# Six temporary tiles, a changed first entry, and q chunks that alternate with gate chunks

## The chip, the cores and the metric

The kernel runs on one core of one Trainium2 chip: one TensorE (PE), one VectorE (DVE), one ScalarE (ACT), one GpSimd (POOL), and SyncE (SP), which issues all the DMAs here. The metric is the device time of one launch in microseconds (us). One profiled execution of the kernel before gives the spans, waits and durations that are quoted.

## The reference

The model has four layers on 1040 tokens (16 meta tokens and 1024 tokens of x) of width 1024. Layers 0 and 3 are sliding-window attention, layer 1 is an mLSTM, layer 2 is an HGRN2 (a gated linear recurrence). Each layer normalizes, runs its mixer, and adds to the residual:

```python
for i in range(DEPTH):
    u = rmsnorm(h, norm_gain[i])
    if kind == 0: y = attention_branch(u, ...)
    elif kind == 1: y = mlstm_branch(u, ...)
    else: y = hgrn2_branch(u, ...)
    h = h + jnp.where(valid[None, :, None], y, 0.0)
```

The change touches the first norm, attention and HGRN2. Attention has 16 query heads of 64 on 4 key heads, a window of 128, a learned sink for each head, and a gate z:

```python
q, k, v, z = _split(u @ w_in, (A_W, A_KVW, A_KVW, A_W))
q = rope(rmsnorm(q.reshape(bsz, lp, A_HEADS, A_HD), q_gain), pos)
k = rope(rmsnorm(k.reshape(bsz, lp, A_KV, A_HD), k_gain), pos)
o = sliding_window_attention(q, k, v, sinks, valid)
return (o * jax.nn.silu(z)) @ w_out
```

In HGRN2 a state S of 128 x 128 for each of 8 heads runs through the tokens; a block's output is `q*exp(A) @ S` plus `att @ v` inside the block, and S then becomes `exp(A_last) * S + (k*exp(A_last - A))^T @ v`.

## The kernel before, in words

**Tiling.** The residual x and the normalized u lie transposed: 8 k-tiles of 128 channels by 1040 tokens. Tokens come in three chunks, `(0,400), (400,384), (784,256)`; attention and the recurrences go by 9 blocks of 16 and 8 x 128 tokens. A product of float32 quality is three fp32r products: each operand is split into a high part and a rest (`split`, L194 to L196: ACT casts, DVE subtracts, L196), and PE adds hi x hi, hi x lo and lo x hi. `proj` (L245 to L269) does so for 128 output channels: for each chunk four steps of six matmuls (L262), and with the last step of a chunk an `evac` that takes the sum out of PSUM.

**What sets the order.** The order on PE is written by hand. A step is `[nominal cost, function, weight load]`; lists of steps are laid into each other by `weave` (two lists at even pace), `spread` and `later` (a step at a nominal time), and `chain` (a step some nominal nanoseconds after the matmuls it follows, also into the next list). A function issues all its work on all engines. PE keeps the hand-written order; the instructions of ACT, DVE, POOL and SP are ordered by the framework's scheduler. SP has one DMA queue that goes in order.

**Pools.** `tmp()` hands out tiles of 404 columns, called `t`, and there are five (`TMPS`). `row()` gives one of 8 rows of 1040 columns, `vtile()` one of 10 small v tiles. An instruction that writes a tile waits until the last reader of its former content is done.

**Norm** (L371 to L425). `sq` squares one k-tile of a chunk (ACT, L377) and adds it up (DVE, L381); `stat` sums over the channels by a matmul with a tile of ones (L389), and `rstd_from` makes the inverse root (ACT, Ln L361 and Exp L362); `unit` scales one k-tile (DVE, L415) and splits it into `uh` and `ul`. In the first layer each chunk is summed in two halves, each with its own stat. The ones and the identity for transposes come in one DMA (`const`).

**Attention** (`layer_a`, from L445). A q or k chunk takes three t tiles, `dst`, `sq` and `rot` (the k chunks of the first half use rows). `evac` (L518 to L527) loads cos and sin into the one tile `cs` (L520), scales into `dst` (ACT, L523), squares into `sq` (ACT, L524), and copies `dst` into `rot` with its halves exchanged by four DMAs (L527). Then follow, at the nominal distances `D_Q` of 2000, 4000 and 6000: `stat`, the norm over 64 channels by a matmul with `masks` (L533); `rope` (DVE, L538 to L541); and the split (for q L492 and L493, for k L473 to L476), which is the last reader of the t tiles. The split of q writes one of four buffers (`qs`) for each chunk; where it would come ahead of the S step of the previous pair that last reads that buffer, the last loop of `layer_a` moves it behind that S step.

Pairs of q tiles go through S steps (scores, L624 and L625; DVE adds the mask and takes the maximum, L630; ACT Exp, L633; POOL divides by the sum, L637), T steps (transposes of the scores, L648) and V steps (L667). There are four segments of these steps, one for each pair of q tiles, and each is woven with a `fill`: the projections that will be needed next. `gate_proj` (L436) projects a chunk of z, makes its silu in one t tile (`sigmoid_from`) and multiplies it onto the attention's output row. `proj_out` (L345, L348) is the output product of two tiles.

```python
fills = [
    [tile_of(vg0, vfin0)] + q_pair(1),
    [zs[0], (out1, [(-Y_AHEAD, z) for z in sp1])] + q_pair(2),
    [tile_of(kg1, kfin1), tile_of(vg1, vfin1), zs[1]] + q_pair(3) + [(out3[:cut], ...)],
    [(out3[cut:], []), zs[2]],
]
```

Here `zs[p]` is the gates of pair p, `out1` and `out3` are output products, `kg1` is the k tile of the second half of the key heads, and `q_pair(p)` gives for each chunk both q tiles of pair p.

**HGRN2** (`layer_c`). For each head and each pair of blocks: level steps on DVE and ACT, then the level products on PE (`levels_mm`, L1127 and L1137), then `tail0` (ACT and DVE take the products out, POOL copies parts into `att`, L1165), `tail1` (transposes of k, L1187) and for each of the two blocks `tail2`, called a V step here: `att` times v (L1202), S times q (L1204), k times v (L1209), and the new S by DVE (L1214). The tails of a pair come `TAIL_LAG` = 600 nominal nanoseconds into the list of the next pair.

**Entry.** The first layer's norm of chunk 0 comes alone; the norms of chunks 1 and 2 lie in the projections of chunks 0 and 1, at the shares in `FIRST`. q tiles 0 and 1 and k are projected chunk by chunk ahead of the first S step (`head`); in the first layer all three chunks of q tile 1 come in the third.

Of the kernel before, what the change touches and what calls it, by code (L numbers as in the profile page):

```python
# [15 lines left out]
P = 128  # L16
# [16 lines left out]

C_IDENT, C_ONES = 0, 128
C_W = 256
B_COLS = 96
LOOKAHEAD = 12000.0
TAIL_LAG = 600.0
PRIO = 40
ROWS, TMPS, RAWS, YS = 8, 5, 2, 3  # L40
XS = 14
# [70 lines left out]
def hybrid_kernel(ctx: ExitStack, tc: tile.TileContext, ins, out, layers=(0, 1, 2, 3)):  # L112
# [13 lines left out]
    def nm(x):  # L126
        ctr[0] += 1
        return f"{x}{ctr[0]}"
# [26 lines left out]

    const = cpool.tile([P, C_W], F32, name="const")
    ident = const[:, C_IDENT : C_IDENT + P]
    ones = const[:, C_ONES : C_ONES + P]
    ngain = cpool.tile([P, 4, KT], F32, name="ngain")
# [15 lines left out]
    load_x(0)  # L175
    sp.dma_start(const, ins["const"])
    sp.dma_start(ngain, ins["ngain"])
# [193 lines left out]
    class Norm:  # L371
        def __init__(self, i):
            self.i, self.acc, self.ps = i, {}, {}

        def sq(self, m, n, c0, cn, size=KT):
            q = tmp()[:, :cn]
            s.activation(q, x[:, m, c0 : c0 + cn], AF.Square)  # L377
            if m % size == 0:
                self.acc[n] = q
            else:  # L380
                v.tensor_tensor(self.acc[n], self.acc[n], q, op=ALU.add)  # L381

# [11 lines left out]

        def stats(self, n, parts):

            c0, cn = CHUNKS[n]
            size = KT // parts

            def squares(part):  # L400
                def fn():
                    for m in range(part * size, (part + 1) * size):
                        self.sq(m, n, c0, cn, size)

                return [0.0, fn, None]

            return [z for k in range(parts) for z in (squares(k), self.stat(n, k, parts))]

# [36 lines left out]
    def layer_a(i, j, first, last, fin):  # L445
# [69 lines left out]
        def qk_proj(src, gcol, work, fsplit, ch):  # L515
            late = {}

            def evac(acc, n, c0, cn):  # L518
                cos_sin = R["mix"].tile([P, 2, 400], F32, tag="cs", name=nm("cs"), bufs=1)
                sp.dma_start(cos_sin[:, :, :cn], ins["rope"][:, :, c0 : c0 + cn].rearrange("a p t -> p a t"))  # L520
                dst, sq, rot = work(n, c0, cn)
                late[n] = dst, sq, rot, cos_sin
                s.activation(dst, acc[:, :cn], AF.Identity, scale=R["cons"][:, gcol : gcol + 1])  # L523
                s.activation(sq, acc[:, :cn], AF.Square)  # L524
                for q in range(4):
                    o = q ^ 1
                    sp.dma_start(rot[32 * q : 32 * q + 32], dst[32 * o : 32 * o + 32])  # L527

            def finish(n, c0, cn):
                def stat():  # L530
                    dst, sq, rot, _ = late[n]
                    st = psa()
                    pe.matmul(st[:, :cn], R["masks"][:, 0:P], sq, start=True, stop=True)  # L533
                    rstd_from(st, sq, cn, 64)
# [195 lines left out]
        cut = len(oc[3][0][1]) + 2  # L730
        zs = [(flat(z_pair(p)), []) for p in range(3)]
# [553 lines left out]
    steps = []  # L1285
    norm = Norm(layers[0])

    steps += norm.stats(0, PARTS[0]) + [norm.unit(0, k) for k in range(KT)]
    tail = None
    for pos, i in enumerate(layers):  # L1290
# [30 lines left out]
        else:  # L1321
            h0, h1 = (sum(z[0] for z in head[k]) for k in range(2))
            seq = flat(head)
            for n, t0, t1, end in ((2, h0 + h1 * FIRST[2], h0 + h1 * FIRST[3], h0 + h1), (1, h0 * FIRST[0], h0 * FIRST[1], h0)):
                st = norm.stats(n, PARTS[n])
                later(seq, *((t0 + (t1 - t0) * k / len(st), z) for k, z in enumerate(st)), *norm.units(n, t1, end))
            head = [seq]
# [8 lines left out]
    steps[k][2] = None  # L1336
    load_x(1)
    k = 0
    for n, (cost, fn, pre) in enumerate(steps):
# [30 lines left out]
def _layout(inp):  # L1370
# [3 lines left out]
    f["ngain"] = np.asarray(inp["norm_gain"]).reshape(4, KT, P).transpose(2, 0, 1)  # L1374
    const = np.zeros((P, C_W), np.float32)
    const[:, C_IDENT : C_IDENT + P] = np.eye(P)
    const[:, C_ONES : C_ONES + P] = 1.0
    am = np.zeros((P, 384), np.float32)
# [6 lines left out]
    f["b_mask"] = np.where(ii <= np.arange(P)[None], 0.0, BIG).astype(np.float32)  # L1385
    f["const"] = const
    half = 32
# [76 lines left out]
```

## Time and profile before

| quantity | value |
|---|---|
| median of 3 runs | 2697.6 us (2693.47 to 2699.81) |
| the profiled execution's own time | 2690.46 us |
| its span | 2688.7 us |
| PE busy (matmuls) | 2590.5 us, 96% of the span |
| PE weight loads (PEld), beside the matmuls | 2492.4 us, 93% |
| DVE busy | 1959.5 us, 73% |
| ACT busy | 1693.4 us, 63% |
| POOL busy | 370.1 us, 14% |
| granted TensorE clock, mean | 0.986 |
| moved by DMA | 145.66 MB |

The profiled execution is 7.1 us below the median, or 0.27%. Rows of single instructions give the start in us, the duration in us, the engine, the line, the operation, `out<-in`, the shapes, and in brackets the engine's idle time just ahead and what ended it. Rows of stretches give the length, then busy us and the number of instructions for PE, PEld, DVE, ACT and POOL, then granted clock, DMA share and GB/s. Rows of waits by line, `PE pa L389 <- DVE t L381: 7.0, 2, 4.0`, give the total wait in us, how many, and the longest. Names such as `t`, `r` (a row), `pa`, `pj`, `po`, `pt` (PSUM tiles), `wr`, `wh`, `wl` (weights raw, high, low) are those of the program.

### The profile page before, as it was taken

How to read it: one execution, taken by the hardware profiler on the slowest of the kernel's cores; microseconds unless marked ns; L12 is line 12 of the kernel's file. 1: busy time of each engine (PE TensorE's matmuls, PEld its weight loads, DVE VectorE, ACT ScalarE, POOL GpSimd, SP SyncE). 2: the span in 40 equal slices, each digit the busy share in tenths (PEclk: the TensorE clock that was granted, in tenths of full speed). 3: DMA queues.
4: the chain of work that ended last, by engine and by line, in shares of the span. 5: the costliest groups of instructions: out<-in, count | busy, mean ns of one | idle time of the engine just before them, and what ended most of it. 6: DMA issues, size and time to landing. Idle time of an engine off the chain costs nothing.

```text
span 2688.7 us, 54502 instructions
## 1 busy us (share of the span) xinstructions
PE 2590.5 (96%) x20276; PEld 2492.4 (93%) x20276; DVE 1959.5 (73%) x5337; ACT 1693.4 (63%) x4339; POOL 370.1 (14%) x760
## 2 busy tenths in 40 slices
PE   6899999999999999999999999999999998998999
PEld 5898989999999999999999998999999898898999
DVE  7787687974646474747475688978878978886886
ACT  7776777565454545454545657877676857766772
POOL 0343243000000000000000000101000000541450
PEclk8999999999999999999999999999999999999999
DMA  4223111011111111111111111101111013212212
GB/s 148 84 59 96 52 58 46 21 65 56 40 56 40 56 40 56 40 56 40 56 40 53 51 34 33 34 33 34 41 33 39 31 45 107 69 53 88 73 36 75
DMA packets 89786, 145.66 MB, mean 54 GB/s; under 512 B 12448, under 2 KB 42272, under 8 KB 89520
## 3 DMA queue, kind: packets, MB, share of 16 engines
q1 hardware_dynamic: 89520, 142.17, 16.9%
q8 instruction: 160, 2.62, 0.4%
q14 instruction: 106, 0.87, 0.1%
HBM read 127.28 MB, written 4.26 MB: 49 GB/s over the span
## 4 chain that ended last, share of the span: by engine, by line
PE 72%; DVE 12%; ACT 8%; issue 3%; POOL 2%; DMA 2%; SPq 0%; ACTq 0%; DVEq 0%; POOLq 0%
PE pj L262 35%; PE pj L345 14%; PE pj L307 9%; ACT Sm L633 1%; PE po L667 1%; PE pt L648 1%; PE po L890 1%; POOL Sm L637 1%; PE pa L904 1%; PE po L892 1%; DVE t L415 1%; DVE ul L196 1%; DVE Sm L630 1%; DVE x L348 1%; PE pj L303 1%
## 5 line engine op out<-in xcount | busy, mean ns | idle before, releaser
L262 PE MATMUL pj<-uh,wh 128*128 128x256 f32 (+2 forms) x2688 | 930.5, 346 | 3.4 <-ACT uh L195 3.4
L262 PE MATMUL pj<-ul,wh 128*128 128x256 f32 (+2 forms) x2688 | 871.7, 324 | 3.2 <-DVE ul L196 3.1
L262 PE MATMUL pj<-uh,wl 128*128 128x256 f32 (+2 forms) x2688 | 869.6, 324 | 0.0
L262 PEld LDWEIGHTS pj<-uh,wh 128*128 128x128 f32 x2688 | 513.4, 191 | 24.3 <-issue 6.4
L262 PEld LDWEIGHTS pj<-ul,wh 128*128 128x128 f32 x2688 | 513.7, 191 | 15.2 <-DVE ul L196 5.3
L262 PEld LDWEIGHTS pj<-uh,wl 128*128 128x128 f32 x2688 | 513.2, 191 | 0.1
L637 POOL TENSOR_SCALAR Sm<-Sm,s 128x256 f32<-128x256 f32 (+2 forms) x272 | 254.5, 947 | 410.7 <-DVE s L635 406.0
L196 DVE TENSOR_TENSOR wl<-wr,wh 128x512 fp32r<-128x512 f32 x336 | 228.7, 690 | 54.1 <-ACT wh L195 51.8
L195 ACT CAST wh<-wr 128x512 fp32r<-128x512 f32 x336 | 201.9, 616 | 97.9 <-PE pj L345 27.1
L348 DVE TENSOR_TENSOR x<-x,pj 128x384 f32<-128x384 f32 (+2 forms) x480 | 234.7, 510 | 38.8 <-PE pj L345 37.1
L345 PE MATMUL pj<-yh,wh 128*128 128x384 f32 (+2 forms) x768 | 252.9, 329 | 0.0
L345 PE MATMUL pj<-yl,wh 128*128 128x384 f32 (+2 forms) x768 | 248.0, 323 | 3.3 <-DVE yl L196 3.3
L345 PE MATMUL pj<-yh,wl 128*128 128x384 f32 (+2 forms) x768 | 246.6, 321 | 0.0
L307 PE MATMUL pj<-wh,uh 128*128 128x256 f32 x768 | 231.0, 301 | 0.0
L307 PE MATMUL pj<-wh,ul 128*128 128x256 f32 x768 | 216.4, 282 | 0.0
L307 PE MATMUL pj<-wl,uh 128*128 128x256 f32 x768 | 216.1, 281 | 0.0
L633 ACT ACTIVATE Sm<-Sm,s 128x257 f32<-128x257 f32 (+2 forms) x272 | 130.6, 482 | 84.6 <-DVE s L630 75.5
L432 DVE SCALAR_TENSOR_TENSOR t<-pj,t 128x384 f32<-128x384 f32 (+2 forms) x192 | 99.0, 515 | 107.0 <-ACT t L431 106.5
L433 ACT ACTIVATE t<-t 128x384 f32<-128x384 f32 (+2 forms) x240 | 117.8, 491 | 80.1 <-DVE t L432 79.0
L345 PEld LDWEIGHTS pj<-yl,wh 128*128 128x128 f32 x768 | 145.1, 189 | 5.7 <-DVE yl L196 5.2
L195 ACT CAST yh<-r 128x384 fp32r<-128x384 f32 (+2 forms) x120 | 57.3, 479 | 143.8 <-PE pj L345 126.2
L345 PEld LDWEIGHTS pj<-yh,wh 128*128 128x128 f32 x768 | 145.3, 189 | 1.7 <-DVE S L1214 0.3
(235 smaller groups left out, 5470.9 us busy)
## 6 DMA issues: line engine op xcount, KB each, us to landing
wr<-in_b_win SPq DMA_DIRECT2D x128, 256.0 KB, 2.9
wr<-in_a_win SPq DMA_DIRECT2D x80, 256.0 KB, 2.9
wr<-in_c_win SPq DMA_DIRECT2D x64, 256.0 KB, 2.8
cs<-in_rope SPq DMA_DIRECT2D x28, 384.0 KB, 3.3
wr<-in_a_wout SPq DMA_DIRECT2D x32, 256.0 KB, 2.7
wr<-in_b_wout SPq DMA_DIRECT2D x32, 256.0 KB, 2.7
cs<-in_rope SPq DMA_DIRECT2D x20, 256.0 KB, 2.7
t<-t SPq DMA_DIRECT2D x104, 48.0 KB, 2.2
```

The source lines that it names most:

```text
L195: s.copy(h, src)
L196: v.tensor_tensor(l, src, h.bitcast(F32), op=ALU.subtract)
L262: pe.matmul(acc[:, :cn], a[:, k, :], b[:, k, c0 : c0 + cn], start=(k == 0 and i == 0), stop=(k == KT - 1 and i == 2))
L303: pe.matmul(acc[:48, :256], um[0][:, k, :], m[:, kk, :], start=(k == 0 and m is wh), stop=(k == KT - 1 and m is wl))
L307: pe.matmul(acc[:cn, :256], a[:, k, c0 : c0 + cn], m[:, kk, :], start=(k == 0 and i == 0), stop=(k == KT - 1 and i == 2))
L345: pe.matmul(acc[:, :cn], a[:, k, mc], b, start=(k == 0 and i == 0), stop=(k == 1 and i == 2))
L348: v.tensor_tensor(x[:, m, c0 : c0 + cn], x[:, m, c0 : c0 + cn], acc[:, :cn], op=ALU.add)
L415: v.scalar_tensor_tensor(u, x[:, k, cs], ngain[:, self.i, k : k + 1], self.acc[n], op0=ALU.mult, op1=ALU.mult)
L432: v.scalar_tensor_tensor(a[:, :cn], z, 0.0, a[:, :cn], op0=ALU.min, op1=ALU.subtract)
L433: s.activation(a[:, :cn], a[:, :cn], AF.Exp)
L633: s.activation(Sm[:nq, u, : nk + 1], Sm[:nq, u, : nk + 1], AF.Exp, scale=-1.0, bias=st[:nq, u : u + 1], accum_out=den[:nq, u : u + 1])
L637: g.tensor_scalar(Sm[:nq, u, :nk], Sm[:nq, u, :nk], den[:nq, u : u + 1], None, op0=ALU.mult)
```

## The change

There are six edits in one:

- `TMPS` goes from 5 to 6.
- In segments 1 and 2 of attention the fills use `qz_pair`: each q chunk of pair 2 (or 3) is followed by one gate chunk of pair 0 (or 1). The output product, which stood ahead of the q chunks, now comes behind them.
- The load of `cs` moves from `evac` to the `stat` step of each q or k chunk (L529 of the new file), that is behind the four copies of that chunk.
- `TAIL_LAG` goes from 600 to 2000.
- In the first layer the norm of chunk 0 is summed in four parts instead of two. Those of chunks 1 and 2 are summed in one part each, seven adds on POOL into a row; `FIRST` now holds for each chunk the shares of its squares, its stat and its first unit. The chunks of q tile 1 join the chunks of k and q tile 0. `ones` is made by a memset, and the identity is loaded behind the second part of x.
- In the later norms the sum of chunk 2 lies in a v tile instead of a t tile.

```diff
-TAIL_LAG = 600.0
+TAIL_LAG = 2000.0
-ROWS, TMPS, RAWS, YS = 8, 5, 2, 3
+ROWS, TMPS, RAWS, YS = 8, 6, 2, 3
-PARTS = 2, 2, 2
-FIRST = 0.3, 0.9, 0.3, 0.7
+PARTS = 4
+FIRST = (0.2, 0.8, 0.85), (0.2, 0.75, 0.8)
...
         def sq(self, m, n, c0, cn, size=KT):
-            q = tmp()[:, :cn]
+            if m % size:
+                q = tmp()[:, :cn]
+            elif self.row is not None and n:
+                q = self.row[:, c0 : c0 + cn]
+            else:
+                q = (vtile() if n == 2 else tmp())[:, :cn]
             s.activation(q, x[:, m, c0 : c0 + cn], AF.Square)
             if m % size == 0:
                 self.acc[n] = q
             else:
-                v.tensor_tensor(self.acc[n], self.acc[n], q, op=ALU.add)
+                (v if self.row is None or n == 0 else g).tensor_tensor(self.acc[n], self.acc[n], q, op=ALU.add)
...
             def evac(acc, n, c0, cn):
-                cos_sin = R["mix"].tile([P, 2, 400], F32, tag="cs", name=nm("cs"), bufs=1)
-                sp.dma_start(cos_sin[:, :, :cn], ins["rope"][:, :, c0 : c0 + cn].rearrange("a p t -> p a t"))
...
                 def stat():
-                    dst, sq, rot, _ = late[n]
+                    dst, sq, rot = late[n]
+                    cos_sin = R["mix"].tile([P, 2, 400], F32, tag="cs", name=nm("cs"), bufs=1)
+                    sp.dma_start(cos_sin[:, :, :cn], ins["rope"][:, :, c0 : c0 + cn].rearrange("a p t -> p a t"))
+                    late[n] = dst, sq, rot, cos_sin
...
+        def qz_pair(p, z):
+            (ga, fa), (gb, fb) = qg[2 * p], qg[2 * p + 1]
+            gates = [grp for t in (2 * z, 2 * z + 1) for grp in zc[t]]
+            res = []
+            for n in range(3):
+                for k, (grp, fin) in enumerate(((ga[n], fa[n]), (gb[n], fb[n]))):
+                    res += [tile_of([grp], [fin]), (gates[2 * n + k], [])]
+            return res
...
-            if n == 2:
+            if first:
+                parts += [tile_of([qb[0][n]], [qb[1][n]])]
+            elif n == 2:
                 parts += [tile_of(*qb)]
...
-            [zs[0], (out1, [(-Y_AHEAD, z) for z in sp1])] + q_pair(2),
-            [tile_of(kg1, kfin1), tile_of(vg1, vfin1), zs[1]] + q_pair(3) + [(out3[:cut], [(-Y_AHEAD, z) for z in sp3])],
-            [(out3[cut:], []), zs[2]],
+            qz_pair(2, 0) + [(out1, [(-Y_AHEAD, z) for z in sp1])],
+            [tile_of(kg1, kfin1), tile_of(vg1, vfin1)] + qz_pair(3, 1) + [(out3[:cut], [(-Y_AHEAD, z) for z in sp3])],
+            [(out3[cut:], []), (flat(z_pair(2)), [])],
...
     load_x(1)
+    sp.dma_start(ident, ins["ident"])
```

Three places show how instructions move. A number behind a name counts the tiles; numbers of the two kernels don't correspond.

The first place is PE in the entry, around the first norm matmul of chunk 1 (`pa_235<-t_218,const`). In the kernel before, 24 projection matmuls of chunk 0 stand ahead of it (`pj_211` and `pj_198` are sums of k and q tile 0):

```order
L262 MATMUL pj_211<-uh,wh_112 128x400
L262 MATMUL pj_211<-ul,wh_112 128x400
L262 MATMUL pj_211<-uh,wl_113 128x400
L389 MATMUL pa_235<-t_218,const 128x384
L262 MATMUL pj_198<-uh,wh_94 128x400
L262 MATMUL pj_198<-ul,wh_94 128x400
```

In the changed kernel 60 stand ahead of it: k, q tile 0, and half of q tile 1 (`pj_301`), and the norms of k and q of chunk 0 (L532, with `masks`) come earlier than it:

```order
L259 MATMUL pj_301<-ul,wh_125 128x400
L259 MATMUL pj_301<-uh,wl_126 128x400
L532 MATMUL pa_316<-r_272,masks_205 128x400
L532 MATMUL pa_322<-t_293,masks_205 128x400
L391 MATMUL pa_326<-r_95,ones 128x384
L259 MATMUL pj_301<-uh,wh_125 128x400
```

So the first sum of chunk 1, which now comes from a row (`r_95`) that POOL adds up, is asked for 36 matmuls later, and there is one such matmul instead of two.

The second place is SP in the first attention layer, at the k tile of the second half, where `cs` is the load of cos and sin and each `x4` is the four rotated copies of a chunk. Before, each load stands ahead of its chunk's copies:

```order
L520 DMA cs_3158<-in_rope 128x2x400
L527 DMA t_3162<-t_3160 32x400 x4
L240 DMA wr_3690<-in_a_win 128x512
L240 DMA wr_3694<-in_a_win 128x512
L520 DMA cs_3214<-in_rope 128x2x384
L527 DMA t_3218<-t_3216 32x384 x4
L520 DMA cs_3254<-in_rope 128x2x256
L527 DMA t_3258<-t_3256 32x256 x4
```

In the changed kernel (the load for the first chunk stands earlier):

```order
L523 DMA t_3177<-t_3175 32x400 x4
L237 DMA wr_3352<-in_a_win 128x512
L523 DMA t_3217<-t_3215 32x384 x4
L529 DMA cs_3262<-in_rope 128x2x384
L523 DMA t_3255<-t_3253 32x256 x4
L529 DMA cs_3307<-in_rope 128x2x256
```

The copies of the second chunk now stand ahead of its load of `cs`, and those of the third chunk ahead of theirs.

The third place is PE in HGRN2, at the V steps of a pair of blocks (`po` is the output, `pa` the new part of S). Before, the first block's step is followed by other work (`um` is the meta tokens' part of a projection); the second block's step comes 36 rows later, behind the level products of the next pair:

```order
L1202 MATMUL po_20290<-att_18666,v_18794 128x128
L1204 MATMUL po_20290<-X_20424,S_20294 128x128
L1209 MATMUL pa_20529<-v_18794,kT_20473 128x128
L303 MATMUL pj_20533<-wh_20360,um_18628 48x256
L303 MATMUL pj_20533<-wl_20361,um_18628 48x256
```

In the changed kernel the two steps of a pair stand together:

```order
L1212 MATMUL po_20386<-att_18666,v_18869 128x128
L1214 MATMUL po_20386<-X_20657,S_20643 128x128
L1219 MATMUL pa_20853<-v_18869,kT_20759 128x128
L1212 MATMUL po_20857<-att_18666,v_18953 128x128
L1214 MATMUL po_20857<-X_20657,S_20855 128x128
L1219 MATMUL pa_20860<-v_18953,kT_20759 128x128
L304 MATMUL pj_20864<-wh_20375,uh 128x256
```

Both steps moved behind the level products of the next pair. The second step's product with S reads `S_20855`, which DVE makes from `pa_20853`, two matmuls after that one.

More of the change, by code (lines that the diff above doesn't have):

```diff
@@ L154, in hybrid_kernel @@
     s.preload_act_table_set("natural_log_exp_and_others")
-    const = cpool.tile([P, C_W], F32, name="const")
-    ident = const[:, C_IDENT : C_IDENT + P]
-    ones = const[:, C_ONES : C_ONES + P]
+    ident = cpool.tile([P, P], F32, name="ident")
+    ones = cpool.tile([P, P], F32, name="ones")
+    v.memset(ones, 1.0)
     ngain = cpool.tile([P, 4, KT], F32, name="ngain")
@@ L175, in hybrid_kernel @@
     load_x(0)
-    sp.dma_start(const, ins["const"])
     sp.dma_start(ngain, ins["ngain"])
@@ L393, in stat, with squares, fn @@
             return [4 * cn * MM, fn, None]
-        def stats(self, n, parts):
-            c0, cn = CHUNKS[n]
+        def squares(self, n, part=0, parts=1):
             size = KT // parts
[L400 to L407, printed above, removed]
+            def fn():
+                for m in range(part * size, (part + 1) * size):
+                    self.sq(m, n, *CHUNKS[n], size)
+            return [0.0, fn, None]
         def unit(self, n, k):
@@ L1285, in hybrid_kernel @@
     steps = []
-    norm = Norm(layers[0])
-    steps += norm.stats(0, PARTS[0]) + [norm.unit(0, k) for k in range(KT)]
+    norm = Norm(layers[0], row())
+    for k in range(PARTS):
+        steps += [norm.squares(0, k, PARTS), norm.stat(0, k, PARTS)]
+    steps += [norm.unit(0, k) for k in range(KT)]
     tail = None
@@ L1385, in _layout @@
     f["b_mask"] = np.where(ii <= np.arange(P)[None], 0.0, BIG).astype(np.float32)
-    f["const"] = const
+    f["ident"] = np.eye(P, dtype=np.float32)
     half = 32
```

18 lines of the change are left out of this document (6 added, 12 removed).

## The prediction

> **What bounds the kernel now.** I read the stretches first: one row per stage, with the busy time of each engine (count in brackets), then the granted TensorE clock, the DMA share and GB/s. The stages are the entry, the rest of the first attention layer, mLSTM (with the seams beside it), HGRN2, and the last attention layer.
>
> ```profile
> 0.00:87.30 87.30, 60.71 (x272) 51.42 (x273) 61.49 (x127) 60.78 (x129) 1.73 (x9) 0.88 0.49 150
> 87.30:520.00 432.70, 411.82 (x2726) 395.54 (x2725) 347.94 (x952) 302.48 (x817) 155.56 (x298) 0.98 0.19 57
> 520.00:1600.00 1080.00, 1075.07 (x7058) 1043.12 (x7057) 667.91 (x1678) 571.09 (x1334) 7.68 (x67) 1.00 0.15 47
> 1600.00:2170.00 570.00, 553.30 (x7040) 528.14 (x7039) 477.99 (x1553) 421.83 (x1197) 56.01 (x129) 0.99 0.12 38
> 2170.00:2690.00 520.00, 489.59 (x3189) 474.19 (x3187) 404.16 (x1030) 337.19 (x863) 149.10 (x257) 0.98 0.22 67
> ```
>
> TensorE is the bound, and mLSTM has 5 us to give. Outside it PE idles 26.6, 20.9, 16.7 and 30.4 us, 95 in all. The change keeps the PE work nearly equal, so it can win only this idle time and the clock lost beside it. So the waits of PE come next, the longest ones of the attention layers first. All are the 64-wide norm of q or k (L533) waiting for ACT's square (L524):
>
> ```profile
> 152.40 1.22 PE L533 MATMUL pa<-t,masks 128*128 128x256 f32 x2 [2.88 <-ACT t L524]
> 252.47 0.48 PE L533 MATMUL pa<-t,masks 128*128 128x256 f32 x1 [3.12 <-ACT t L524]
> 270.65 0.79 PE L533 MATMUL pa<-t,masks 128*128 128x256 f32 x1 [4.77 <-ACT t L524]
> 360.70 0.80 PE L533 MATMUL pa<-t,masks 128*128 128x256 f32 x1 [3.77 <-ACT t L524]
> 2243.49 0.59 PE L533 MATMUL pa<-r,masks 128*128 128x384 f32 x1 [2.05 <-ACT r L524]
> 2274.28 0.48 PE L533 MATMUL pa<-t,masks 128*128 128x256 f32 x1 [3.98 <-ACT t L524]
> 2343.44 0.48 PE L533 MATMUL pa<-t,masks 128*128 128x256 f32 x1 [1.63 <-ACT t L524]
> 2438.32 0.48 PE L533 MATMUL pa<-t,masks 128*128 128x256 f32 x1 [3.86 <-ACT t L524]
> 2458.07 0.80 PE L533 MATMUL pa<-t,masks 128*128 128x256 f32 x1 [4.77 <-ACT t L524]
> 2544.67 0.68 PE L533 MATMUL pa<-t,masks 128*128 128x256 f32 x1 [2.42 <-ACT t L524]
> ```
>
> All but 2243.49 are a third chunk (256 wide), after two chunks that have already filled the five t tiles. The timeline before 270.65, the third chunk of the second k tile, shows why:
>
> ```profile
> 265.31 0.57 DVE L539 TENSOR_TENSOR t<-t,cs 128x400 f32<-128x400 f32 x1
> 265.90 0.38 SPq L520 DMA_DIRECT2D cs<-in_rope  x1
> 266.51 2.41 SPq L527 DMA_DIRECT2D t<-t  x4
> 269.56 0.57 DVE L475 TENSOR_TENSOR r<-t,r 64x400 fp32r<-64x400 f32 x1 [1.31 <-ACT r L473]
> 270.21 0.38 ACT L524 ACTIVATE t<-pj 128x256 f32<-128x256 f32 x1
> 270.56 0.56 DVE L538 TENSOR_TENSOR t<-t,cs 128x384 f32<-128x384 f32 x1 [0.43 <-DMA t<-t]
> ```
>
> The square starts 0.08 us after the split of the first chunk (L475, 269.56 to 270.13) frees its tile. And a rotation takes 5.25 us from L539 to the next L538: the only cs tile is loaded when L539 has read it, and the four rotated copies stand behind that load on SP. Chunks come faster, so tiles run out at the third.
>
> A long wait also halves the clock afterwards (stretches that start where a wait ends):
>
> ```profile
> 82.26:87.23 4.97, 4.97 (x14) 4.62 (x15) 1.59 (x3) 0.90 (x2) 0.00 (x0) 0.50 0.35 106
> 270.65:274.96 4.31, 4.31 (x12) 4.09 (x13) 3.16 (x6) 3.27 (x7) 0.00 (x0) 0.50 0.30 84
> 360.70:363.70 3.00, 3.00 (x10) 2.81 (x11) 1.79 (x5) 0.89 (x2) 2.40 (x2) 0.50 0.43 113
> 1668.24:1674.40 6.16, 6.16 (x127) 5.66 (x128) 3.54 (x13) 2.73 (x11) 0.00 (x0) 0.50 0.01 3
> ```
>
> Half of each is lost: 2.5, 2.2, 1.5 and 3.1 us. I count 1.5 for a wait whose stretch isn't shown.
>
> [...]
>
> **The change, part by part.** The sum is made against the profiled execution, 2690.46 us (span 2688.7, 1.8 around it); the median of the runs, 2697.6, is 0.27% longer, and I scale by that.
>
> *Alternation (q pairs 2 and 3, both layers).* Twelve q and gate chunks change places; the work is the same. After each q chunk a gate chunk of similar length follows, which needs one t tile for a short time and nothing that PE waits for. q chunks come half as often, some 11 us apart where a rotation takes 5.25. The waits 3.12, 3.77, 3.86 and 2.42 (13.2) and three clock stretches (4.5) can go: 17.7. The output product that stood ahead comes later, and its gates have been done long before. I take -15, ends -18 and -5.
>
> *Six t tiles, later cs load, k of the second half.* Its three chunks now follow an output product, which holds no t tile, and two chunks fit in six tiles. On SP the copies of the second and third chunk no longer stand behind the cs load. 2 x (4.77 + 2.2) = 13.9 is there; the third chunk still waits for some tile of the first. -11, ends -14 and -4.
>
> *q pair 1 and the head of the last layer.* Here only the sixth tile helps, since SP's order stays as it was: 2.88, 1.63, 2.05 and 3.98 with three stretches, 15 in all. A sixth tile covers one of the three that a chunk takes: -5, ends -12 and +2.
>
> *Entry.* The waits of PE there, and the price of the adds that move:
>
> ```profile
> PE pa L389 <- DMA const<-in_const: 8.6, 1, 8.6
> PE pa L389 <- DVE t L381: 7.0, 2, 4.0
> PE pa L533 <- ACT t L524: 5.0, 3, 3.9
> L415 DVE SCALAR_TENSOR_TENSOR t<-x,ngain,t 128x384 f32<-128x384 f32 x8 | 4.5, 616 | 3.8 <-ACT t L362 3.8
> L196 DVE TENSOR_TENSOR ul<-t,uh 128x384 fp32r<-128x384 f32 x8 | 4.0, 556 | 0.0
> L381 DVE TENSOR_TENSOR t<-t,t 128x384 f32<-128x384 f32 x6 | 3.2, 555 | 0.3
> L637 POOL TENSOR_SCALAR Sm<-Sm,s 128x256 f32<-128x256 f32 x224 | 224.6, 1014 | 208.4 <-DVE s L635 203.9 <-PE pt L648 3.8
> L637 POOL TENSOR_SCALAR Sm<-Sm,s 128x144 f32<-128x144 f32 x32 | 23.1, 733 | 128.6 <-DVE s L635 128.5
> ```
>
> Without the wait for const the first norm still needs the eighth square and its matmul: -0.5. Chunks 1 and 2 put seven adds each in a chain on POOL. No POOL add is in the trace: DVE's 0.56 is the low end; the two POOL rows give 2.5 ns an element, 1.34 us at 384; twice that slope gives 2.3. I take 1.34, the same engine: the chain ends some 9.4 us after the second square (about 22), at 31.4, where PE, with q1's first half ahead of it now, comes at about 28. Chunk 2: seven at 1.01 against the work of three tiles, some 1 us. So 7.0 becomes 4.4. Units still feed PE at 1.17 us each (616 + 556) in both kernels. The 3.9 us at 82 and its stretch of 2.5 go, as q1 is spread over the chunks; rope steps that DVE takes before the last unit cost 2. Together -0.5 - 2.6 - 3.9 - 2.5 + 2 = -7.5; I take -7. Ends: -15 (adds at DVE's price), +4 (2.3 us each).
>
> [...]
>
> *HGRN2 tails.* TAIL_LAG places the V steps of a block pair later, behind the level products of the next pair. What waits there now, and how fast the state S follows:
>
> ```profile
> PE po L1202 <- POOL att L1165: 16.0, 10, 3.5
> 1833.39 0.38 PE L1202 MATMUL po<-att,v 128*128 128x128 f32 x1 [3.25 <-POOL att L1165]
> 1705.05 0.39 PE L1209 MATMUL pa<-v,kT 128*128 128x128 f32 x2
> 1705.48 0.35 DVE L1214 SCALAR_TENSOR_TENSOR S<-S,s,pa 128x128 f32<-128x128 f32 x1 [0.17 <-PE pa L1209]
> 1824.45 0.39 PE L1209 MATMUL pa<-v,kT 128*128 128x128 f32 x2
> 1827.89 0.34 DVE L1214 SCALAR_TENSOR_TENSOR S<-S,s,pa 128x128 f32<-128x128 f32 x1
> ```
>
> PE gets more projection work ahead of the first V step, mostly 3 us and more, so nine of the ten waits for att go; that at 1833, a last pair, moves least: about 2 of the 16.0 stay. The clock of this stage, 0.99 over 553 us, gives some 5 back. But the two V steps of a pair now stand next to each other or a few matmuls apart, and the second needs the S of the first: a new wait, 32 times. S is there 0.39 us after its matmul (1705.44 to 1705.83), or 3.39 us (1824.84 to 1828.23) when other work is ahead of it on DVE. With the short one the cost is 1; with the long one now and then, up to 20; I take 6, nearer the short one, as it is what the rows show where the steps stand close. -14 - 5 + 6 = -13, ends -20 and +2.
>
> *New waits.* The split of an early q chunk is held until the previous pair's S step has read its buffers, so its t tile is held too: two held, three in use, one for a gate. It just fits. +4, ends 0 and +15. The v tile for the norm's third chunk and the separate ident load lie under mLSTM's dense PE work or behind x: 0.
>
> Sum: -15 - 11 - 5 - 7 - 13 + 4 = -47, so 2643.5, scaled 2650.
>
> **Rivals.** *Half comes back:* the two short chains that the change makes, adds on POOL and V steps on S, cost their upper ends: entry +4, HGRN2 14 worse, -22, scaled 2675. For it: DVE is 84% busy in HGRN2 (478 of 570), so S queues. Against: 1705. Chance 0.22.
>
> *Everything goes:* all low ends, -79, scaled 2618. Against: ACT and DVE are 70% busy in the entry and don't vanish. 0.10.
>
> *It does not do what it says:* tiles held by splits keep q and k waiting as now (31 not won), and S takes 12 more than taken: -4, scaled 2694. 0.04.
>
> *Slower, by held t tiles:* if seven were needed, the last q chunk of a pair would wait not for a rotation but for the S step that frees a split. [...] It decides when the rotation of one chunk is not done before the next q chunk ends. Against: that distance is about 10 us. 0.06.
>
> **How the numbers follow.** The forecast, 2630 to 2668 on its own, has 0.58. Faster by over 0.2% (5 us, about what a measurement of this kernel can tell) are it and the first two rivals: 0.90; within: 0.04; slower: 0.06. The range 2620 to 2684 takes in the forecast, most of the first rival and half of the second: 0.8.
>
> **What would show it.** Right: the L524 waits of pairs 2 and 3 and of the second k are gone or under 1.5 us, with clock 1.00 there; PE reaches the first S product near 80 us instead of 87.3; waits for att under 3 us in all. Wrong: POOL adds above 1.8 us; waits of L1214 for S above 10 us in all; a wait for tiles in the alternated stretch of over 5 us, which would put it above 2697.

## The result, and the profile after

| | before | changed |
|---|---|---|
| median | 2698.04 us (2693.47 to 2699.81, 4 runs) | 2653.50 us (2652.86 to 2658.61, 4 runs) |
| profiled execution: time, span | 2690.46, 2688.7 us | 2652.86, 2651.1 us |
| PE busy, PE idle in the span | 2590.5, 98.2 us | 2578.8, 72.3 us |
| granted TensorE clock | 0.986 | 0.995 |

The ratio is 0.9842, with a 95% interval of 0.9824 to 0.9859: 44.5 us faster by the medians, forecast 47.6. The two profiled executions lie only 37.6 us apart, since that of before (2690.46) was shorter than all runs of its median. What follows is worked out from those 37.6. They are 25.9 us less idle time of PE and 11.7 us less PE time for the same matmuls. I put the latter down to the clock (0.986 before, 0.995 now), though not in the entry, where PE time rose by 3.8 us at a clock of 0.92 instead of 0.88.

To see where they fall, both traces are cut at the same six instructions: first S product, last output product of layer 0, first of the last output products of mLSTM, the last of these, first output product behind HGRN2, first S product of the last layer. The columns are the length, then busy us (count) of PE, PEld, DVE, ACT and POOL, then granted clock, DMA share and GB/s. Before:

```profile
0.00:87.26 87.26, 60.67 (x270) 51.38 (x271) 61.49 (x127) 60.78 (x129) 1.73 (x9) 0.88 0.49 150
87.26:509.07 421.81, 401.29 (x2670) 385.48 (x2669) 337.49 (x927) 294.62 (x800) 155.56 (x298) 0.98 0.19 56
509.07:1555.94 1046.87, 1042.66 (x6857) 1011.05 (x6856) 639.18 (x1620) 560.13 (x1312) 6.96 (x65) 1.00 0.15 49
...
1603.80:2174.51 570.71, 554.01 (x7039) 528.53 (x7038) 475.30 (x1547) 422.64 (x1199) 56.01 (x129) 0.99 0.12 38
2174.51:2279.60 105.09, 96.91 (x560) 92.50 (x559) 90.49 (x194) 65.39 (x145) 0.54 (x4) 0.97 0.27 77
2279.60:2688.70 409.10, 388.18 (x2599) 377.50 (x2598) 312.60 (x835) 268.40 (x712) 148.56 (x253) 0.98 0.22 66
```

The changed kernel:

```profile
0.00:83.94 83.94, 64.44 (x271) 51.56 (x271) 57.19 (x108) 57.28 (x122) 14.59 (x23) 0.92 0.45 138
83.94:498.11 414.17, 399.20 (x2670) 381.94 (x2669) 338.21 (x934) 296.84 (x808) 158.00 (x297) 1.00 0.21 61
498.11:1542.42 1044.31, 1040.56 (x6858) 1009.74 (x6857) 638.60 (x1620) 559.62 (x1312) 7.33 (x66) 1.00 0.16 50
...
1590.11:2149.83 559.72, 548.74 (x7040) 525.67 (x7038) 472.82 (x1547) 421.43 (x1199) 54.10 (x128) 1.00 0.12 38
2149.83:2252.10 102.27, 94.58 (x560) 89.56 (x559) 88.90 (x192) 65.00 (x142) 0.79 (x5) 1.00 0.27 77
2252.10:2651.10 399.00, 384.65 (x2599) 374.18 (x2598) 313.49 (x838) 268.49 (x714) 148.56 (x253) 1.00 0.23 68
```

The entry wins 3.3 us, the first attention body 7.6, HGRN2 11.0, the head of the last layer 2.8, its body 10.1. The other 2.7 lie in mLSTM (2.6) and its seam, where nothing was forecast. I call the two bodies and the head of the last layer the attention parts: 936.0 us before, 915.4 now.

What PE waits for, summed over the kernel (total us, times, longest; selected rows), before:

```profile
PE pa L533 <- ACT t L524: 37.3, 15, 4.8
PE po L1202 <- POOL att L1165: 16.0, 10, 3.5
...
PE pj L262 <- ACT uh L195: 3.4, 4, 2.5
...
PE pj L345 <- DVE yl L196: 3.3, 6, 0.8
```

and in the changed kernel, where L532 is the norm of q or k, L342 the output product, L259 a projection, L1214 the product with S and L580 the transposes of v:

```profile
PE pj L259 <- ACT uh L192: 9.2, 7, 3.8
PE pj L342 <- DVE yl L193: 8.9, 10, 3.3
...
PE pa L532 <- ACT t L520: 7.7, 5, 3.3
...
PE po L1214 <- DVE S L1224: 5.8, 11, 1.4
PE pt L580 <- ACT t L573: 4.2, 2, 2.2
```

Most of the waits that the change was expected to remove are gone: 37.3 became 7.7, all of it in the last layer (5.9 in its head), and the 16.0 for att became 0.8. About 15 us came back in three places behind the entry: the output product waits for its split (8.9 instead of 3.3), V steps wait for S (5.8), and the transposes of v wait for ACT (4.2). A fourth is the entry, where projections wait for u (9.2 instead of 3.4). In one of the experiments below, the sixth tile alone beside the rest, the profiled execution took 9259.60 us, 3.5 times as long as usual; its trace isn't used, and its time is that of its other three runs.

### The profile page after: what moved, and what is told of

Its sections match the earlier page's. It is cut to its first block, busy times and chain, and to the rows that moved or that the text cites. A ratio compares the mean times of both kernels' runs of the same rounds, so it can differ in the third digit from the quotient of the medians.

```text
span 2651.1 us, 54484 instructions
## 1 busy us (share of the span) xinstructions
PE 2578.8 (97%) x20276; PEld 2478.5 (93%) x20276; DVE 1952.1 (74%) x5324; ACT 1690.1 (64%) x4339; POOL 384.1 (14%) x774
## 4 chain that ended last, share of the span: by engine, by line
PE 71%; DVE 15%; ACT 7%; DMA 3%; issue 2%; POOL 1%; SPq 1%; DVEq 0%; ACTq 0%; POOLq 0%
PE pj L259 34%; PE pj L342 14%; PE pj L304 9%; PE po L666 1%; PE pt L647 1%; DMA cs<-in_rope 1%; PE po L900 1%; PE pa L914 1%; DVE t L413 1%; PE po L902 1%; ACT Sm L632 1%; DVE ul L193 1%; DVE x L345 1%; POOL Sm L636 1%; DVE wl L193 1%
## 5 line engine op out<-in xcount | busy, mean ns | idle before, releaser
L259 PE MATMUL pj<-uh,wh 128*128 128x256 f32 (+2 forms) x2688 | 924.1, 344 | 9.4 <-ACT uh L192 9.2
L259 PE MATMUL pj<-ul,wh 128*128 128x256 f32 (+2 forms) x2688 | 869.1, 323 | 3.1 <-DVE ul L193 2.8
L259 PE MATMUL pj<-uh,wl 128*128 128x256 f32 (+2 forms) x2688 | 865.7, 322 | 0.0
L259 PEld LDWEIGHTS pj<-uh,wh 128*128 128x128 f32 x2688 | 510.4, 190 | 30.4 <-ACT uh L192 13.4
L259 PEld LDWEIGHTS pj<-ul,wh 128*128 128x128 f32 x2688 | 511.3, 190 | 16.5 <-DVE ul L193 7.2
L259 PEld LDWEIGHTS pj<-uh,wl 128*128 128x128 f32 x2688 | 510.9, 190 | 0.0
L342 PE MATMUL pj<-yl,wh 128*128 128x384 f32 (+2 forms) x768 | 246.5, 321 | 8.9 <-DVE yl L193 8.9
L342 PE MATMUL pj<-yh,wh 128*128 128x384 f32 (+2 forms) x768 | 252.2, 328 | 2.0 <-DVE t L438 1.0
L342 PE MATMUL pj<-yh,wl 128*128 128x384 f32 (+2 forms) x768 | 245.6, 320 | 0.0
L342 PEld LDWEIGHTS pj<-yl,wh 128*128 128x128 f32 x768 | 144.8, 189 | 12.0 <-DVE yl L193 11.6
L342 PEld LDWEIGHTS pj<-yh,wh 128*128 128x128 f32 x768 | 144.3, 188 | 5.3 <-DVE x L345 2.1
```

Source lines behind the costliest of these rows:

```text
L259: pe.matmul(acc[:, :cn], a[:, k, :], b[:, k, c0 : c0 + cn], start=(k == 0 and i == 0), stop=(k == KT - 1 and i == 2))
L342: pe.matmul(acc[:, :cn], a[:, k, mc], b, start=(k == 0 and i == 0), stop=(k == 1 and i == 2))
```

## The experiments

Each kernel is given with its median, and its ratio to the kernel before with the 95% interval.

**One part undone.** The first four take one part out of the changed kernel.

```diff
-TAIL_LAG = 2000.0
+TAIL_LAG = 600.0
```

> The changed kernel with TAIL_LAG back at 600. Theory (each part pays for its own waits): the waits for att in HGRN2 come back, about 15 us in all, and the clock of that stage falls back to 0.99, while the short waits for S go; HGRN2, now 559.7 us, goes back to 569 to 572, and the kernel to about 2664 (2660 to 2667). Rival (the HGRN2 gain came from elsewhere, as from the sixth t tile, which also holds the squares of its norm): HGRN2 stays under 563 and the kernel under 2657.

Measured: 2665.75 us, 0.9882 (0.9864 to 0.9899). HGRN2 took 569.69 us, and the waits for att were back at 17.0 us in ten. The theory holds: TAIL_LAG is worth 12 us here, 10.0 of them in HGRN2 by the traces. On top of the sixth tile alone, further below, it is worth about the same.

```diff
-            qz_pair(2, 0) + [(out1, [(-Y_AHEAD, z) for z in sp1])],
-            [tile_of(kg1, kfin1), tile_of(vg1, vfin1)] + qz_pair(3, 1) + [(out3[:cut], ...)],
+            [zs[0], (out1, [(-Y_AHEAD, z) for z in sp1])] + q_pair(2),
+            [tile_of(kg1, kfin1), tile_of(vg1, vfin1), zs[1]] + q_pair(3) + [(out3[:cut], ...)],
```

> The changed kernel with the fills of before (gates, output product, then the q chunks of a pair one behind the other), all else kept. Theory (alternation and tiles share the work): two of three chunks fit in six tiles, so the waits of the third chunk of q pairs 2 and 3 come back in part, 1 to 2.5 us each instead of 2.4 to 3.9 before, with one or two half-clock stretches; the new wait of 3.3 us at 230, where four splits of q run at once behind an S step, goes. Net 2 to 8 us slower: 2656 to 2662. Rival 1 (the sixth tile and the later load do it all): no such wait, and the kernel is 2 to 5 us faster, about 2650. Rival 2 (alternation does it all): all of 17.7 us comes back, 2670.

Measured: 2654.79 us, 0.9845 (0.9827 to 0.9862), attention parts 915.7 us. The theory's range begins at 2656, and the first rival has 2650; the alternation brings nothing that can be measured once there are six tiles. The wait of 3.3 at 230 went, but others of 1.8 and 2.7 us for the same split (of y, for the output product) came at 360 and 2518.

```diff
-ROWS, TMPS, RAWS, YS = 8, 6, 2, 3
+ROWS, TMPS, RAWS, YS = 8, 5, 2, 3
```

> The changed kernel with five t tiles. Theory: the waits of the k tile of the second half come back (4.8 and 3.8 to 4.8 us with half-clock stretches of some 2 us each), and so do those of q pair 1 and of the last layer's head, some 3 to 5 us more each; in the alternated stretches held tiles add 0 to 5. 10 to 18 us slower: 2664 to 2672. Rival (the later load of cos and sin does it, and the sixth tile is spare): within 3 us of 2653.

Measured: 2665.23 us, 0.9883 (0.9866 to 0.9899), attention parts 925.4. The tile is worth 12 us beside the alternation, as the theory has it (2664 to 2672).

The fourth has the first entry of before (two sums for each chunk, adds on DVE, q tile 1 behind the head, ones and identity in one load) and all other edits but the smallest: the sum of chunk 2 in the later norms is back in a t tile too.

```diff
-PARTS = 4
-FIRST = (0.2, 0.8, 0.85), (0.2, 0.75, 0.8)
+PARTS = 2, 2, 2
+FIRST = 0.3, 0.9, 0.3, 0.7
...
-            if first:
-                parts += [tile_of([qb[0][n]], [qb[1][n]])]
-            elif n == 2:
+            if n == 2:
                 parts += [tile_of(*qb)]
```

> The kernel before with all edits but those of the first entry (two sums each of chunks 0 to 2 on DVE, q tile 1 after the head as before, ones and identity in one load). Theory: the first S product comes 3 to 5 us later than in the changed kernel (83.9 us), at 87 to 89, as in the kernel before, and nothing behind it differs: 2656 to 2659. Rival (with six tiles and the later load the old entry loses its wait of 3.9 us at 82 and its half-clock stretch as well): the first S product at 80 to 83, the kernel at 2650 to 2653, so that the entry edits bring nothing of their own.

Measured: 2652.70 us, 0.9834 (0.9819 to 0.9849). The first S product came at 86.56, 2.6 us later than in the changed kernel, where the theory had 3 to 5. But "nothing behind it differs" was wrong: the first attention body took 411.70 instead of 414.17 us. The entry's 2.6 us are given back behind it, and the time is the one that the rival gave for another reason (2650 to 2653).

**The three attention edits one by one.** The undone parts add up to some 12 + 1 + 12 - 1 = 24 of 44.5 us, so parts must stand in for each other. The next four bring the combinations of sixth tile, alternation and later load of cos and sin to seven, all with the new entry and TAIL_LAG 2000; the eighth, with none of the three, was not run. Their edits are those above, and for the early load:

```diff
             def evac(acc, n, c0, cn):
+                cos_sin = R["mix"].tile([P, 2, 400], F32, tag="cs", name=nm("cs"), bufs=1)
+                sp.dma_start(cos_sin[:, :, :cn], ins["rope"][:, :, c0 : c0 + cn].rearrange("a p t -> p a t"))
...
                 def stat():
-                    cos_sin = R["mix"].tile([P, 2, 400], F32, tag="cs", name=nm("cs"), bufs=1)
-                    sp.dma_start(cos_sin[:, :, :cn], ins["rope"][:, :, c0 : c0 + cn].rearrange("a p t -> p a t"))
```

> The changed kernel with the load of cos and sin back ahead of the copies. Stages as sums: the attention parts (last layer's head and both bodies) take 936.0 us before, 915.4 in the changed kernel, 915.7 without the alternation, 925.4 with five tiles. Theory (the three edits stand in for each other: the alternation halves the pace at which q chunks ask for tiles, the sixth tile and the later load raise what is there): only k of the second half and the heads, which don't alternate, lose: attention parts 918 to 921, the kernel 2656 to 2660. Rival (the later load carries the gain together with the tile, and the alternation does nothing in any combination): attention parts 924 to 928, the kernel 2663 to 2667, and the kernel that has the sixth tile alone comes out the same.

> Of the three attention edits the sixth tile alone (early load, old fills), with the rest of the change. Theory (they stand in for each other): the waits of q pairs 2 and 3 that neither alternation nor later load now covers come back at 1 to 3 us each: attention parts 923 to 928, 4 us or more above the kernel that alternates, 2661 to 2667. Rival (the alternation does nothing in any combination): within 2 us of the kernel with tile and alternation and early load.

> Of the three attention edits the later load of cos and sin alone (five tiles, old fills), with the rest of the change. Theory (they stand in for each other): with five tiles the alternation counts, so that this is 4 us or more above the kernel with five tiles and alternation (2665.2): attention parts 929 to 935, 2669 to 2675. Rival (the alternation does nothing in any combination): 924 to 928, 2663 to 2668.

> Of the three attention edits the alternation alone (five tiles, early load), with the rest of the change. Theory (they stand in for each other): q pairs 2 and 3 are covered, k of the second half, q pair 1 and the heads wait as before: attention parts 922 to 930, 2662 to 2670. Rival (the alternation does nothing in any combination): as the kernel before, 936 to 939, 2674 to 2678.

Measured, medians and ratios, with the attention parts from the traces:

| tiles | alternation | load | median us | ratio (95%) | attention parts |
|---|---|---|---|---|---|
| 6 | yes | later | 2653.50 | 0.9842 (0.9824 to 0.9859) | 915.4 |
| 6 | yes | early | 2652.43 | 0.9831 (0.9817 to 0.9846) | 915.6 |
| 6 | no | later | 2654.79 | 0.9845 (0.9827 to 0.9862) | 915.7 |
| 6 | no | early | 2649.82 | 0.9822 (0.9806 to 0.9839) | not used |
| 5 | yes | later | 2665.23 | 0.9883 (0.9866 to 0.9899) | 925.4 |
| 5 | yes | early | 2661.75 | 0.9865 (0.9850 to 0.9880) | 921.6 |
| 5 | no | later | 2683.95 | 0.9951 (0.9935 to 0.9968) | 944.7 |

With six tiles the intervals of the four kernels overlap. With five, the alternation is worth 18.7 us (2683.95 to 2665.23), and without the alternation the sixth tile is worth 29.2 (2683.95 to 2654.79). So tile and alternation stand in for each other, as the theory had it, but not by halves: the tile alone does all. The later load gains in none of the three pairs of rows: it stands 1.1, 5.0 and 3.5 us above the early one, each time with intervals that overlap. The numbers of the theory missed all four times: it had 2656 to 2660 and 2661 to 2667 for the two kernels with six tiles and the early load, 2669 to 2675 for the later load alone, and 2662 to 2670 for the alternation alone, which missed by 0.25 us. Its rival, that the alternation never counts, fell with the kernels of five tiles.

The same order shows in one line of the waits by line, the norm of q or k, in the kernels with five tiles. Later load alone, later load with alternation, alternation alone:

```profile
PE pa L532 <- ACT t L520: 36.0, 12, 4.8
```

```profile
PE pa L532 <- ACT t L520: 19.9, 10, 3.7
```

```profile
PE pa L531 <- ACT t L522: 19.4, 10, 3.7
```

Five tiles leave 36 us without the alternation and 19 to 20 with it; six left 7.7.

**Starting from before.** The last four put the parts that pay into the kernel before.

```diff
-ROWS, TMPS, RAWS, YS = 8, 5, 2, 3
+ROWS, TMPS, RAWS, YS = 8, 6, 2, 3
```

> The kernel before with the sixth t tile and nothing else. Theory (the sixth tile alone takes the attention waits away; alternation and later load stand beside it for nothing): attention parts 912 to 917 us instead of 936.0, HGRN2 569 to 572 as before, 2660 to 2666. Rival (the sixth tile needs one of the other edits, or the entry edits, beside it): attention parts over 922, 2669 or more.

Measured: 2658.78 us, 0.9861 (0.9845 to 0.9878), attention parts 910.0, HGRN2 571.76, entry 82.20. One number of the six edits brings 37.8 us (the kernel before took 2696.53 beside it), 1.2 us beyond the theory's range. Its waits:

```profile
PE po L1202 <- POOL att L1165: 16.4, 10, 3.4
PE pa L533 <- ACT t L524: 10.6, 9, 3.9
...
PE pj L345 <- DVE yl L196: 6.4, 8, 2.7
```

The timeline of this kernel at the third chunk of the second k tile, the place that the prediction shows at 265 to 271 us, shows there why one tile is enough (selected rows):

```profile
253.79 0.57 DVE L540 TENSOR_TENSOR t<-t,t 128x400 f32<-128x400 f32 x1
254.40 0.47 ACT L523 ACTIVATE t<-pj,cons 128x256 f32<-128x256 f32 x1 [0.66 <-DVE t L540]
254.88 0.57 DVE L541 TENSOR_TENSOR t<-t,t 128x400 f32<-128x400 f32 x1
255.48 0.38 ACT L524 ACTIVATE t<-pj 128x256 f32<-128x256 f32 x1 [0.61 <-DVE t L541]
255.92 0.70 PE L533 MATMUL pa<-t,masks 128*128 128x256 f32 x2 [1.45 <-ACT t L524]
257.11 0.56 DVE L475 TENSOR_TENSOR r<-t,r 64x400 fp32r<-64x400 f32 x1
```

The first and the second chunk now hold all six tiles. The third chunk's `dst` takes the `rot` of the first when L540 has read it, and its `sq` takes the `sq` of the first, 0.03 us after L541 (255.45 to 255.48). With five tiles its square had to wait for a further tile, `dst` of the first chunk, which the split (L475) reads last. The split comes only at 257.11 and 258.17 here, behind ACT's casts. So the sixth tile doesn't cover a third of the shortage: it moves what the third chunk waits for from the split's end to the rope's end, and the 4.77 us shrink to 1.45.

```diff
-TAIL_LAG = 600.0
+TAIL_LAG = 2000.0
```

(beside the sixth tile)

> The kernel before with the sixth t tile and TAIL_LAG 2000, two numbers of the change and nothing else. Theory (these two are all that pays, and the rest nets nothing): HGRN2 559 to 561, attention parts 912 to 917, entry 86 to 88, 2648 to 2654, no slower than the whole change (2653.5). Rival (entry and alternation pay some us that single removals do not show, since one covers for the other): 2656 to 2662.

Measured: 2649.22 us, 0.9824 (0.9809 to 0.9839), entry 82.70, attention parts 909.5, HGRN2 560.15. The theory holds: two numbers give all that the whole change gives. Only its stages are a little off, the entry (86 to 88) and the attention parts (912 to 917) came out shorter. The four other edits add nothing; that they cost the 4.3 us by which the medians differ isn't shown, as the intervals overlap.

```diff
-TAIL_LAG = 600.0
+TAIL_LAG = 1200.0
```

(beside the sixth tile)

> The kernel before with the sixth t tile and TAIL_LAG 1200, half way. In half of the pairs the first V step now stands behind the next pair's level products, and the second one right behind it. Theory (the waits for att go in proportion to the work put ahead of the first V step): of the 16 us of waits for att some 5 to 9 are left, waits for S are 2 to 4, HGRN2 563 to 567, 2653 to 2659. Rival (it needs the whole lag, as the long waits are those of the pairs that move last): HGRN2 568 or more, 2660 to 2664.

Measured: 2659.47 us, 0.9864 (0.9850 to 0.9879), HGRN2 570.44: no gain over 600, against the theory's 563 to 567. But the rival's reason is wrong too. The waits of PE in HGRN2 were

```profile
PE po L1204 <- DVE S L1214: 12.2, 8, 2.6
PE po L1202 <- POOL att L1165: 3.6, 7, 1.1
```

so the waits for att did go, and those for S took their place. The timeline shows one, with the first V step's product for S (L1209) and the product that needs the new S (L1204):

```profile
1712.58 0.39 PE L1209 MATMUL pa<-v,kT 128*128 128x128 f32 x2
...
1714.61 0.48 DVE L1111 TENSOR_TENSOR X<-r,r 128x128 f32<-128x128 f32 x2
1715.01 0.48 DVE L1112 TENSOR_TENSOR X<-r 128x128 f32<-128x128 f32 x2
1715.41 0.33 DVE L1214 SCALAR_TENSOR_TENSOR S<-S,s,pa 128x128 f32<-128x128 f32 x1
...
1715.80 0.49 PE L1204 MATMUL po<-X,S 128*128 128x128 f32 x2 [2.61 <-DVE S L1214]
```

S could start at 1712.97 and starts 2.44 us later, behind level steps of the next pair that DVE took first. At 2000 5.7 us of these waits are left; that the V steps then meet DVE at a better place among the level steps is argued, not shown.

The last one is a candidate: a gap of 800 nominal ns between the two V steps of a pair, and k's copies across the partitions on POOL for the second half, both on the kernel with sixth tile and TAIL_LAG 2000.

```diff
+                    if b:
+                        ts.append([800.0, lambda: None, None])
                     ts.append(S(640, tail2, r, b))
...
-                        s.copy(kh[os, cs], k[hs])
+                        (g.tensor_copy if j else s.copy)(kh[os, cs], k[hs])
...
-                        s.copy(kl[os, cs], kl[hs, cs].bitcast(F32))
+                        (g.tensor_copy if j else s.copy)(kl[os, cs], kl[hs, cs].bitcast(F32))
```

> A candidate: the kernel before with the sixth t tile, TAIL_LAG 2000, a gap of 800 nominal ns between the two V steps of a pair, and for the k tile of the second half the copies to the other half of the partitions on POOL instead of ACT. Theory: the gap takes away the waits for S (5.8 us in all with the whole change) without bringing back those for att: HGRN2 555 to 558; the evacuation of v no longer stands behind a row of ACT casts, and the wait of 2.0 to 2.2 us of the transposes of v goes in both layers: attention parts 2 to 4 us less than with the sixth tile and the lag alone. 2641 to 2648. Rival (the copies on POOL are slower by more than ACT gains, and k is there too late for the S steps of pair 2; the second V step, put later, keeps PSUM and att longer): attention parts longer by 3 us or more, HGRN2 unchanged, 2652 to 2660.

Measured: 2650.83 us, 0.9827 (0.9813 to 0.9842): nothing gained, where the theory had 2641 to 2648. In HGRN2 (562.33 us) fewer V steps wait for S, but longer, and some wait for att again:

```profile
PE po L1204 <- DVE S L1214: 5.9, 5, 1.5
PE po L1202 <- POOL att L1165: 4.4, 4, 1.9
```

The copies on POOL had nothing to win, since without the alternation v's transposes have little to wait for (0.4 us in each layer of the kernel before); attention parts are 908.7 instead of 909.5.

## Why the prediction was right, and where it wasn't

The forecast of 2650 was 3.5 us below the measured 2653.5, inside the range; its likeliest case came true. Its signs of being right showed as well, but for the first S product, which came at 83.9 us where "near 80" was expected: in the alternated stretches and at the second k PE waits at most 1.04 us for the square of a norm of q or k, and the clock is 1.00 but for a stretch at 2433 us (last section). By its terms:

- **Alternation (-15): wrong as an attribution.** The step that failed is "q chunks come half as often", taken as the cause of a gain beside six tiles. With five tiles this is so (18.7 us); with six there was nothing left for it.
- **Third chunks and the sixth tile (-11 and -5): mis-sized.** "A sixth tile covers one of the three that a chunk takes" failed. Alone on the kernel before it brings 26.0 us in the attention parts (936.0 to 910.0) and 5.1 in the entry of the profiled executions, and 37.8 by the medians. The timeline at 254 us shows that the number of tiles was the wrong measure: what counts is which reader frees the tile that the third chunk still lacks.
- **The later load, taken as part of the -11: no gain.** That "the copies of the second and third chunk no longer stand behind the cs load" is what the order shows, but no pair of kernels gains by it. With the old entry and six tiles the first S product comes at 86.56 us with it, and at 82.2 to 84.3 us in the four kernels without it (they differ in other edits too, none of which reaches the entry, and by 2.1 us among themselves, one trace each). That cos and sin, now asked for only with the norm's matmul, are there too late is argued, not shown.
- **Entry (-7): half, then nothing.** The first S product came 3.3 us earlier, but the old entry is as early with six tiles alone (82.20). The 8.6 us for const went without gain: the first projection matmul comes at 14.70 us, before at 14.11. The adds on POOL were cheaper than taken:

```profile
L383 POOL TENSOR_TENSOR r<-r,t 128x384 f32<-128x384 f32 x7 | 7.5, 1069 | 22.9 <-ACT t L379 22.6
L383 POOL TENSOR_TENSOR r<-r,t 128x256 f32<-128x256 f32 x7 | 6.2, 884 | 17.0 <-ACT t L379 16.6
```

  They took 1.07 us instead of 1.34, 1.9 times the 0.56 of DVE for an add of the same size (L381 in the kernel before). The chain of chunk 1 still ended at 31.84 (taken: 31.4), because POOL waited for the squares between its adds, and PE waits 1.5 us for it. What was mis-sized is the term of 2 for rope steps ahead of the last units; the waits for `uh` grew by 5.8 us (3.4 to 9.2):

```profile
40.34 0.62 DVE L413 SCALAR_TENSOR_TENSOR t<-x,ngain,r 128x384 f32<-128x384 f32 x1
...
43.90 0.56 DVE L473 TENSOR_TENSOR r<-r,r 64x400 fp32r<-64x400 f32 x1
44.38 0.56 DVE L540 TENSOR_TENSOR t<-t,t 128x400 f32<-128x400 f32 x1
44.87 0.60 DVE L413 SCALAR_TENSOR_TENSOR t<-x,ngain,r 128x384 f32<-128x384 f32 x1
...
46.84 0.44 PE L259 MATMUL pj<-uh,wh 128*128 128x384 f32 x1 [3.78 <-ACT uh L192]
```

  Two units of chunk 1 are 4.53 us apart, with rope and split of q and k between them, and PE waits 3.8 us for the second; the clock was 0.61 over the next 3.2 us. And the body behind it is 2.5 us longer than behind the old entry: up to 130 us T steps wait 2.4 us for POOL's scores instead of 0.4. That the last chunks' rope and splits are still in the way there is argued, not shown.
- **HGRN2 (-13): right, -11.0.** Term by term: the waits for att went from 16.0 to 0.8 us (forecast: about 2 left), PE time fell by 5.3 at a clock of 1.00 instead of 0.99 (5), the new wait for S is 5.8 (6). What wasn't forecast are 3.7 us of waits for level steps and transposes (2.4 and 1.3).
- **Held tiles (+4): the size, but not the cause.** In the alternated stretch of the first layer PE has no wait for a norm of q at all, so no held tile shows there. The splits moved behind the S step run there all at once instead, on DVE, ahead of the split of y:

```profile
226.05 0.55 DVE L491 TENSOR_TENSOR qs<-t,qs 64x384 fp32r<-64x384 f32 x1
...
226.83 1.91 DVE L491 TENSOR_TENSOR qs<-t,qs 64x384 fp32r<-64x384 f32 x3
...
229.38 0.55 DVE L193 TENSOR_TENSOR yl<-r,yh 128x384 fp32r<-128x384 f32 x1
...
229.99 0.44 PE L342 MATMUL pj<-yl,wh 128*128 128x384 f32 x1 [3.33 <-DVE yl L193]
```

  Four splits of 0.55 to 0.64 us, and PE waits 3.33 us for `yl` behind them. The kernels without the alternation have no such row of splits, but `yl` waits there behind rope and V work of DVE, 2.7 us in the last layer; this fits that undoing the alternation brought nothing back.

That the sum came out so close is in part luck. The gain that I gave to the alternation was the sixth tile's, so that these two errors cancelled. By the profiled executions, on which the sum was made, the change won 37.6 us of 47: less in the attention parts than my terms had (20.6 of 27, held tiles counted) and in the entry (3.3 of 7), while mLSTM and its seam gave 2.7. The medians lie 44.5 apart because that of before was 7.6 us above its profiled execution, and that of the changed kernel 0.6.

## What to carry to other kernels

Where several edits go at one shortage, ask of each what is left of its wait when the others are in, or their gains are counted twice. When a pool is short by one, find the reader that frees the tile that the late user lacks: one more tile moves the wait to an earlier reader, and may be worth all of it. Moving a consumer later on one engine takes away its wait only if what it feeds is not queued behind other work by then: half the lag moved 12 us of waits from att to S and gained nothing.

## What the runs showed of the hardware

In the trace of the changed kernel the length of one wait doesn't tell whether the clock falls behind it. The first three of these stretches start where a wait ends, of 3.33, 2.22 and 2.02 us (granted clock third from the end: 1.00, 1.00 and 0.58), and the next three are in the entry, where no wait of PE was over 0.53 us from 48 us to the fall of the clock (1.00, 0.65 and 0.50):

```profile
229.99:233.00 3.01, 3.01 (x20) 3.01 (x21) 2.68 (x8) 1.10 (x4) 0.10 (x1) 1.00 0.00 0
274.73:277.50 2.77, 2.77 (x19) 2.77 (x20) 1.19 (x3) 1.86 (x6) 0.00 (x0) 1.00 0.02 6
2432.98:2436.00 3.02, 3.02 (x14) 3.02 (x15) 1.04 (x3) 1.67 (x5) 0.00 (x0) 0.58 0.02 5
...
62.00:64.00 2.00, 1.26 (x4) 0.67 (x4) 1.87 (x6) 1.88 (x6) 0.00 (x0) 1.00 0.00 0
64.00:66.00 2.00, 1.73 (x6) 1.13 (x6) 1.93 (x6) 1.95 (x5) 0.00 (x0) 0.65 0.00 0
66.00:68.00 2.00, 1.12 (x3) 0.65 (x3) 1.78 (x5) 0.84 (x3) 0.00 (x0) 0.50 0.49 127
```

The longest wait, of 3.33 us, kept the full clock of 1.00, the shortest of the three, of 2.02 us, came ahead of 0.58, and in the entry the clock fell from 1.00 to 0.65 while PE got only four and six matmuls in 2 us. I had priced the clock by single long waits, and that doesn't hold here. How dense the work just ahead is doesn't settle it in these rows either: PE was busy without a break for the 10 us ahead of both the 2.22 and the 2.02 us, with 64 matmuls each and at a clock of 1.00. What decides isn't shown.
